# Latent attention swept by halves of 512 queries over two score tiles, instead of quarters of 256 over five

## Chip, core and metric

One NeuronCore of one Trainium2 chip runs the whole kernel as a single program. The metric is device time in microseconds, the median of three runs. The engines are TensorE (PE in the profile, its weight loads PEld), VectorE (DVE), ScalarE (ACT), GpSimd (POOL) and SyncE (SP, which here only issues DMAs).

## What is computed

The kernel is a two-layer encoder on 1024 positions of width 1024, in 32-bit floats. Each layer is a token mixer with four groups of heads, an output projection, and a gated MLP with a short convolution. The change touches group C of the mixer alone, dense latent attention with four heads:

```python
def block(args):
    qn, qr = args
    sc = (jnp.einsum('bqhd,bkhd->bhqk', qn, k_nope) + jnp.einsum('bqhr,bkr->bhqk', qr, k_rope)) * scale
    p = jax.nn.softmax(sc, axis=-1)
    return jnp.einsum('bhqk,bkhd->bqhd', p.astype(v.dtype), v)
...
y = jnp.concatenate([oa, ob, oc, od], axis=-1) @ w_out[l]
```

Every query of a head sees all 1024 keys, with head dimension 96 (64 plain, 32 rotary) and values of 64.

## The kernel before

Activations are kept transposed: channels on the 128 partitions, positions along the free dimension. A matmul that needs full precision is made of three (`mm3`, lines 465 to 470): operands are split into a high part, rounded by ScalarE (line 110), and a low part, the difference, made by GpSimd or VectorE (line 111).

Per layer the mixer runs groups A, D, B and C, then `project_out` multiplies the mixer's 1024 channels, as eight tiles of 128, with the output weights. Group C (`group_c`, 943 to 1003) makes keys for two heads at a time (`keys`) and queries for the next head (`queries`), and sweeps each head in four quarters of 256 queries (`attend_c`, 1005 to 1033). A quarter does this:

- Scores of 8 key tiles x 256 queries, with keys on the partitions, two key tiles to a PSUM bank of 512 columns. ScalarE copies each bank to a score tile `s` in SBUF (line 1021), so `s` is 128 x 2048, 8 KB a partition.
- The maximum over all keys: VectorE folds 2048 columns to 1024, 512 and 256 (1023 to 1025), then `gather` (122 to 134) transposes in 32 x 32 blocks, reduces, and folds the four partition groups with tiny instructions (130 to 133); `replicate` (136 to 138) copies the result back to all groups and `spread` (140 to 144) transposes it into a tile `m` of 256 columns.
- `s - m`: VectorE takes key tiles 0 to 3 and 4 to 6, GpSimd takes key tile 7 (line 1032).
- `weigh` (627 to 639): ScalarE exponentiates 512 columns at a time in place (634); TensorE multiplies with the values, into `o` in PSUM (637). Each weighing matmul is recorded as two. A column block of ones among the values gives the denominators, which `denominators` and `normalise` (641 to 660) use once per head: head h - 1 is finished behind the third quarter of head h, and the last head behind its own end, straight into channel tile 5.

There are five score tiles, used in turn: `self.sc[(4 * h + quarter - 11) % 5]`. They share their SBUF space with the mixer's channel tiles, as `open_shared` (241 to 259) lays out: the pair of high and low part of channel tile k takes 8 KB, and the score tiles lie over the pairs of tiles 1, 3, 7, 4 and 5, in the order in which the last quarters leave them. Tiles 6, 2 and 0 lie over the queries' and keys' low parts and a scratch tile. `mixed()` declares the channel tiles there; a channel tile can be loaded from HBM (line 1087, SyncE's queue) when the score tile under it is no longer read.

`project_out` (1076 to 1116) loads and splits the channel tiles in `ORDER_MIX = (0, 1, 6, 2, 3, 7, 4, 5)`, and first accumulates output tiles 0 to 3 of the first 512 positions over them in that order (`products`, tile `pw`): 8 x 4 x 3 = 96 matmuls, in two `pj` and two `psc` banks. Output tiles 4 to 7 and the second half of the positions follow.

The order on each engine is not written by hand. A planner orders the instructions by their place in the program and by when it expects their inputs; each engine then runs its own list in order and waits on semaphores. Two places bind it: score matmuls are kept in program order (`behind`), and temporaries (`ta` for the maxima, `tb` for the transpose, `tc` for `m`, `tn` for the denominators) exist once each. Score banks are `psc`, two of them; the last head uses the two `pj` banks as well.

Of the kernel before, what the change touches and what calls it, by code (L numbers as in the profile page):

```python
# [9 lines left out]
F32 = mybir.dt.float32  # L10
F32R = mybir.dt.float32r
I32 = mybir.dt.int32
AF = mybir.ActivationFunctionType
ALU = mybir.AluOpType
# [6 lines left out]
S = 1024  # L21
# [42 lines left out]
HALVES = (slice(0, 512), slice(512, 1024))  # L64


ORDER_MIX = (0, 1, 6, 2, 3, 7, 4, 5)
# [25 lines left out]
class Trunk:  # L93
# [147 lines left out]
    def open_shared(self, name):  # L241

        self.hctx = ExitStack()
        p = self.hctx.enter_context(self.tc.tile_pool(name=name, bufs=1, reuse_waits="tile", side="right"))
        half = lambda k, i, dt=F32R: p.tile([128, S], dt, name="hx", tag=f"h{'hl'[i]}{k}")
        pair = lambda k, dt=F32R: p.tile([128, 2 * S], dt, name="hp", tag=f"hp{k}")
        first = (6, 2, 0)
        qlc = [half(6, i) for i in range(2)]
        kls = [half(2, 0), half(2, 1), half(0, 0)]
        rt = half(0, 1, F32)  # L250
        sc = [pair(k, F32) for k in (1, 3, 7, 4, 5)]

        def mixed():
            t = {k: [half(k, i) for i in range(2)] if k in first else
                 (lambda q: [q[:, i * S:i * S + S] for i in range(2)])(pair(k)) for k in ORDER_MIX}
            self.hh, self.hl = ([t[k][i] for k in range(KT)] for i in range(2))

        self.mixed = mixed
        return qlc, kls, rt, sc
# [683 lines left out]
    def group_c(self, l, lat, kr, v, wuk, wuq):  # L943
        nc = self.nc
        (qnh, qnl), ((kvh,), (kvl,)) = lat["cq"], lat["ckv"]
        (ukh, ukl), (uqh, uql), (krh, krl) = wuk, wuq, kr

        def keys(i):
            kh = [(self.lp if i and j else self.kp).tile([128, S], F32R, name="kh", tag="ks") for j in range(2)]
            kl = [next(self.kls) for _ in range(2)]  # L950
            for half in range(2):
                hs = HALVES[half]
                pool, tag = (self.pj, "pj") if i else (self.psc, "psc")
                ps = pool.tile([128, 512], F32, name="pk", tag=tag)
                cs = slice(128 * i, 128 * i + 128)
                self.mm3(ps, ukh[:, cs], ukl[:, cs], kvh[:, hs], kvl[:, hs], True, True)
                for j in range(2):
                    src = ps[64 * j:64 * j + 64]
                    nc.scalar.activation(kh[j][0:64, hs], src, AF.Copy)
                    nc.vector.tensor_sub(kl[j][0:64, hs], src, kh[j][0:64, hs].bitcast(F32))  # L960
            for j in range(2):
                nc.scalar.activation(kh[j][64:128, :], krh[64:128, :].bitcast(F32), AF.Copy)
                nc.vector.tensor_copy(kl[j][64:128, :], krl[64:128, :].bitcast(F32))
            return list(zip(kh, kl))

        def queries(h):
            qh = self.qp.tile([128, S], F32R, name="qh", tag="qh")
            ql = self.qlc[h % 2]
            for half in range(2):
                hs = HALVES[half]  # L970
                ps = self.pj.tile([128, 512], F32, name="pj", tag="pj")
                for k in range(2):
                    cs = slice(512 * k + 128 * h, 512 * k + 128 * h + 128)
                    self.mm3(ps, uqh[:, cs], uql[:, cs], qnh[k][:, hs], qnl[k][:, hs], k == 0, k == 1)

                t = self.rt[half]
                nc.vector.tensor_mul(t, ps, self.cs[:, hs])
                self.split(qh[:, hs], ql[:, hs], t, nc.vector if h == 0 else nc.gpsimd)
            return qh, ql

        ks, qs = keys(0), queries(0)
        end = lambda o, dst=None: self.normalise(dst, o[0:64], 1024, 64 if dst is not None else 0,
                                                 self.denominators(o, 1024))
        last = None
        for h in range(4):
            (kh, kl), (qh, ql) = ks[h % 2], qs
            if h == 1:
                ks = keys(1)
            if h < 3:
                qs = queries(h + 1)  # L990
            o = self.po.tile([128, 1024], F32, name="po", tag="po")
            for quarter in range(4):
                self.attend_c(l, h, quarter, kh, kl, qh, ql, v, o)
                if last and quarter == 2:
                    self.store_mix(448 + 64 * h, end(last))
            last = o

        self.mixed()
        t = self.tmp("b")[64:128]
        end(last, t)  # L1000
        for half in range(2):
            hs = HALVES[half]
            self.split(self.hh[5][64:128, hs], self.hl[5][64:128, hs], t[:, hs], nc.vector)

    def attend_c(self, l, h, quarter, kh, kl, qh, ql, v, o):
        nc = self.nc
        q0 = 256 * quarter
        qs = slice(q0, q0 + 256)
        s = self.sc[(4 * h + quarter - 11) % 5]
        pieces = []  # L1010
        for i in range(4):
            pool, tag = (self.pj, "pj") if i > 1 and h == 3 else (self.psc, "psc")
            ps = pool.tile([128, 512], F32, name="psc", tag=tag)
            for u in range(2):
                kt = 2 * i + u
                ts = slice(128 * kt, 128 * kt + 128)
                with self.behind():
                    self.last = self.mm3(ps[:, 256 * u:256 * u + 256], kh[:, ts], kl[:, ts], qh[:, qs],
                                         ql[:, qs], u == 0, True)
                pieces.append((kt, 256 * kt, slice(256 * kt, 256 * kt + 256), qs))  # L1020
            nc.scalar.activation(s[:, 512 * i:512 * i + 512], ps, AF.Copy)
        mx = self.tmp("a")
        nc.vector.tensor_max(mx, s[:, 0:1024], s[:, 1024:2048])
        nc.vector.tensor_max(mx[:, :512], mx[:, 0:512], mx[:, 512:1024])
        nc.vector.tensor_max(mx[:, :256], mx[:, 0:256], mx[:, 256:512])
        r = self.gather(mx[:, :256], 256, ALU.max)
        self.replicate(r, 8)
        m = self.tmp("c")[:, :256]
        self.spread(m, r[:, :8], 8)
        for eng, c0, c1 in ((nc.vector, 0, 4), (nc.gpsimd, 7, 8), (nc.vector, 4, 7)):  # L1030
            s3 = s[:, 256 * c0:256 * c1].rearrange("p (s q) -> p s q", q=256)
            eng.tensor_sub(s3, s3, m.unsqueeze(1).broadcast_to([128, c1 - c0, 256]))  # L1032
        self.weigh(o, v, h, pieces, s, 2048, 96.0 ** -0.5)


    def mixer(self, l):
# [362 lines left out]
```

## Time and profile before

| | us |
|---|---|
| median of three runs | 3239.51 (3237.86 to 3241.6) |
| the profiled execution | 3236.76 |
| its span, first to last instruction | 3234.9 |
| busy in the span: PE | 2985.9 (92%) |
| DVE | 2029.7 (63%) |
| ACT | 1063.9 (33%) |
| POOL | 956.7 (30%) |
| mean granted TensorE clock, share of full speed | 0.974 |

Busy shares are means over stages with different limits, so the stage of the change has to be cut out by its time. In a list by line, "busy, mean ns" is followed by the idle time ahead of the group and what ended it. In a timeline, an idle time in brackets names the engine and line that ended the wait. A line can be that of a helper: line 126 is the transpose of every `gather`, whoever calls it, so groups are told apart by tile and shape.

### The profile page before, as it was taken

What the parts mean: (1) busy time and instruction counts of PE and PEld (TensorE: products, weight loads), DVE (VectorE), ACT (ScalarE), POOL (GpSimd) and SP (SyncE); (2) the same over time, 40 slices, a digit from 0 to 9 for tenths busy, and PEclk for the clock granted to TensorE, in tenths of its full rate; (3) what the DMA queues carried; (4) which work ended last, traced back from release to release, by engine and by line L of the source; (5) the groups of instructions that cost most, each with busy time, mean ns of one, the idle gap of its engine ahead of it and who ended that gap; (6) DMA issues with size and microseconds to landing.
All of it is one profiled execution on the core that took longest, in us unless ns stands there. A gap on an engine that the chain in (4) does not pass through costs nothing. (4 is left out here: it accounts for less than half of the span.)

```text
span 3234.9 us, 35358 instructions
## 1 busy us (share of the span) xinstructions
PE 2985.9 (92%) x13706; PEld 2365.9 (73%) x13706; DVE 2029.7 (63%) x2849; ACT 1063.9 (33%) x1554; POOL 956.7 (30%) x712
## 2 busy tenths in 40 slices
PE   7888988988999999999988998898899999999997
PEld 3677767776677777788856886777676888888886
DVE  6687567698656666653587727568956434434347
ACT  4232443554332222212243324336534222222222
POOL 1221133324342322223232213142334422233222
PEclk9998999999999999999999998999999999999998
DMA  5235111103312433211131121110132111111113
GB/s 202 78 101 177 54 37 34 56 20 108 128 58 93 134 113 114 95 40 52 46 124 58 55 82 42 38 52 19 37 109 91 65 39 40 43 62 52 40 40 104
DMA packets 103091, 237.15 MB, mean 73 GB/s; under 512 B 11227, under 2 KB 29915, under 8 KB 102924
## 3 DMA queue, kind: packets, MB, share of 16 engines
q1 hardware_dynamic: 102924, 234.90, 22.4%
q8 instruction: 107, 1.75, 0.2%
q14 instruction: 60, 0.49, 0.1%
HBM read 205.59 MB, written 32.67 MB: 74 GB/s over the span
## 5 line engine op out<-in xcount | busy, mean ns | idle before, releaser
L111 POOL TENSOR_TENSOR wl<-raw,wh 128x1024 fp32r<-128x1024 f32 (+2 forms) x96 | 234.5, 2451 | 663.7 <-ACT wh L110 472.4
L477 PE MATMUL pj<-hp,uh 128*128 128x512 f32 x880 | 352.6, 401 | 1.6 <-ACT hp L442 1.6
L478 PE MATMUL pj<-hp,uh 128*128 128x512 f32 x880 | 347.1, 394 | 2.9 <-POOL hp L445 2.8
L477 PE MATMUL pj<-hh,wh 128*128 128x512 f32 x800 | 327.9, 410 | 14.2 <-DVE ql L526 8.5
L478 PE MATMUL pj<-hl,wh 128*128 128x512 f32 x800 | 323.2, 404 | 3.7 <-POOL hl L445 3.2
L481 PE MATMUL pj<-hp,ul 128*128 128x512 f32 x880 | 290.2, 394 | 0.0
L111 POOL TENSOR_TENSOR ul<-raw,uh 128x1024 fp32r<-128x1024 f32 x96 | 238.5, 2486 | 162.5 <-PE pj L481 84.7
L875 DVE TENSOR_SCALAR ta<-u,par 128x1024 f32<-128x1024 f32 (+1 forms) x46 | 55.9, 1216 | 356.1 <-ACT u L1128 324.0
L477 PE MATMUL pj<-hx,uh 128*128 128x512 f32 x528 | 212.5, 403 | 12.6 <-ACT u L1128 10.0
L110 ACT ACTIVATE wh<-raw 128x1024 fp32r<-128x1024 f32 (+2 forms) x104 | 107.2, 1047 | 345.1 <-PE po L469 242.8
L481 PE MATMUL pj<-hx,ul 128*128 128x512 f32 x528 | 209.8, 397 | 0.0
L478 PE MATMUL pj<-hx,uh 128*128 128x512 f32 x528 | 207.7, 393 | 0.0
L481 PE MATMUL pj<-hh,wl 128*128 128x512 f32 x800 | 206.5, 398 | 0.0
L477 PEld LDWEIGHTS pj<-hp,uh 128*128 128x128 f32 x880 | 165.6, 188 | 45.6 <-ACT hp L442 2.2
L478 PEld LDWEIGHTS pj<-hp,uh 128*128 128x128 f32 x880 | 165.5, 188 | 44.9 <-POOL hp L445 5.5
L481 PEld LDWEIGHTS pj<-hp,ul 128*128 128x128 f32 x880 | 165.2, 188 | 39.3 <-issue 1.0
L477 PEld LDWEIGHTS pj<-hh,wh 128*128 128x128 f32 x800 | 154.4, 193 | 54.0 <-issue 17.0
L110 ACT ACTIVATE uh<-raw 128x1024 fp32r<-128x1024 f32 x100 | 105.5, 1059 | 262.9 <-DMA raw<-in_w_up_dram 141.2
L1190 DVE TENSOR_TENSOR y<-y,po 128x1024 f32<-128x1024 f32 x96 | 117.0, 1219 | 110.6 <-PE po L470 110.6
L478 PEld LDWEIGHTS pj<-hl,wh 128*128 128x128 f32 x800 | 154.1, 193 | 41.8 <-POOL hl L445 5.4
L481 PEld LDWEIGHTS pj<-hh,wl 128*128 128x128 f32 x800 | 151.6, 190 | 34.6 <-issue 0.2
L1128 ACT ACTIVATE u<-pj 128x512 f32<-128x512 f32 x176 | 103.7, 593 | 209.1 <-PE pj L481 209.1
(375 smaller groups left out, 7120.2 us busy)
## 6 DMA issues: line engine op xcount, KB each, us to landing
raw<-in_w_up_dram SPq DMA_DIRECT2D x88, 512.0 KB, 3.5
mr<-in_w_mod_dram SPq DMA_DIRECT2D x144, 256.0 KB, 3.4
raw<-in_w_in_dram SPq DMA_DIRECT2D x52, 512.0 KB, 3.5
raw<-in_w_down_dram SPq DMA_DIRECT2D x44, 512.0 KB, 3.5
room<-in_w_mod_dram SPq DMA_DIRECT2D x48, 256.0 KB, 3.6
xd<-y SPq DMA_DIRECT2D x48, 256.0 KB, 2.4
raw<-in_w_out_dram SPq DMA_DIRECT2D x16, 512.0 KB, 3.9
x<-xd SPq DMA_DIRECT2D x14, 512.0 KB, 4.4
```

What stands on the lines that cost most here:

```text
L110: self.nc.scalar.activation(hi, src, AF.Copy)
L111: (eng or self.nc.gpsimd).tensor_sub(lo, src, hi.bitcast(F32))
L477: nc.tensor.matmul(ps, wh[:, ks], self.hh[k][:, hs], start=k == 0, stop=False, skip_group_check=True)
L478: nc.tensor.matmul(ps, wh[:, ks], self.hl[k][:, hs], start=False, stop=False, skip_group_check=True)
L481: nc.tensor.matmul(ps, wl[:, ks], self.hh[k][:, hs], start=False, stop=k == KT - 1, skip_group_check=True)
L875: nc.vector.tensor_scalar(o, t[:, 0:n], cw(0), None, op0=ALU.mult)
L1128: nc.scalar.activation(u[:, 1 + 512 * half:513 + 512 * half], ps, AF.Copy)
L1190: self.mark = nc.vector.tensor_add(d, d, p)
```

## The change

Group C sweeps each head in two halves of 512 queries. A score tile becomes 128 x 4096 (16 KB a partition), and there are two, one for each half of a head. One key tile's scores fill a bank. The maxima are folded as the scores come: after key tile 3 (two blocks of 1024 columns), after 5 and after 7 (one more each), then 1024 to 512. `gather`, `replicate` and `spread` run on 512 queries. VectorE subtracts key tiles 0 to 1, 2 to 3 and 4 to 6, GpSimd key tile 7, now 512 columns. The finished head h - 1 is normalised behind the first half of head h. In the last head only key tiles 5 and 7 use the `pj` banks. The score tiles lie over channel tiles (1, 3) and (7, 4); tile 5 has space of its own.

```diff
-        pair = lambda k, dt=F32R: p.tile([128, 2 * S], dt, name="hp", tag=f"hp{k}")
-        first = (6, 2, 0)
+        quads = ((1, 3), (7, 4))
+        quad = lambda i, dt=F32R: p.tile([128, 4 * S], dt, name="hq", tag=f"hq{i}")
...
-        sc = [pair(k, F32) for k in (1, 3, 7, 4, 5)]
+        sc = [quad(i, F32) for i in range(2)]
...
         def mixed():
-            t = {k: [half(k, i) for i in range(2)] if k in first else
-                 (lambda q: [q[:, i * S:i * S + S] for i in range(2)])(pair(k)) for k in ORDER_MIX}
+            t = {k: [half(k, i) for i in range(2)] for k in (0, 6, 2, 5)}
+            for i, ks in enumerate(quads):
+                q = quad(i)
+                for j, k in enumerate(ks):
+                    t[k] = [q[:, at * S:at * S + S] for at in (2 * j, 2 * j + 1)]
...
-            for quarter in range(4):
-                self.attend_c(l, h, quarter, kh, kl, qh, ql, v, o)
-                if last and quarter == 2:
+            for half in range(2):
+                self.attend_c(l, h, half, kh, kl, qh, ql, v, o)
+                if last and half == 0:
...
+        hs = HALVES[half]
+        s = self.sc[half]
+        pieces, mx = [], self.tmp("a")
+        for kt in range(8):
+            pool, tag = (self.pj, "pj") if kt > 3 and kt % 2 and h == 3 else (self.psc, "psc")
             ps = pool.tile([128, 512], F32, name="psc", tag=tag)
+            ts, cs = slice(128 * kt, 128 * kt + 128), slice(512 * kt, 512 * kt + 512)
+            with self.behind():
+                self.last = self.mm3(ps, kh[:, ts], kl[:, ts], qh[:, hs], ql[:, hs], True, True)
+            nc.scalar.activation(s[:, cs], ps, AF.Copy)
+            pieces.append((kt, 512 * kt, cs, hs))
+            if kt == 3:
+                nc.vector.tensor_max(mx, s[:, 0:1024], s[:, 1024:2048])
+            elif kt in (5, 7):
+                nc.vector.tensor_max(mx, mx, s[:, 512 * kt - 512:512 * kt + 512])
         nc.vector.tensor_max(mx[:, :512], mx[:, 0:512], mx[:, 512:1024])
...
+        r = self.gather(mx[:, :512], 512, ALU.max)
+        self.replicate(r, 16)
+        m = self.tmp("c")[:, :512]
+        self.spread(m, r[:, :16], 16)
+        for eng, c0, c1 in ((nc.vector, 0, 2), (nc.gpsimd, 7, 8), (nc.vector, 2, 4), (nc.vector, 4, 7)):
+            s3 = s[:, 512 * c0:512 * c1].rearrange("p (s q) -> p s q", q=512)
+            eng.tensor_sub(s3, s3, m.unsqueeze(1).broadcast_to([128, c1 - c0, 512]))
+        self.weigh(o, v, h, pieces, s, 4096, 96.0 ** -0.5)
```

## Rows read from the trace of the kernel before

**Rows 1.** Two stretches, busy us (count): PE, PEld, DVE, ACT, POOL; clock; DMA
```profile
630.00:770.00 140.00, 118.70 (x653) 95.22 (x653) 133.54 (x241) 78.74 (x141) 37.70 (x30) 0.96 0.10 29
2210.00:2350.00 140.00, 118.78 (x653) 95.08 (x652) 133.45 (x241) 78.62 (x141) 37.51 (x30) 0.96 0.10 29
```

**Rows 2.** Timeline, PE: start us, us, line, op, tiles [idle before <-releaser]
```profile
777.26 3.69 PE L637 MATMUL po<-hp,v 128*96 128x256 f32 x16 [1.66 <-ACT hp L634]
...
792.88 0.50 PE L469 MATMUL pw<-hp,wh 128*128 128x512 f32 x1 [2.03 <-POOL hp L111]
```

**Rows 3.** Stretches, instructions on pw alone: PE, PEld, ACT busy us (count)
```profile
626.00:780.60 154.60, 11.50 (x43) 7.91 (x44) 0.00 (x0) 0.97 0.12 37
780.60:796.00 15.40, 13.37 (x55) 10.43 (x56) 1.79 (x4) 1.00 0.59 187
```

**Rows 4.** DVE by line and shape, 626 to 772 us: busy us, mean ns
```profile
L1032 DVE TENSOR_TENSOR hp<-hp,tc 128x1024 f32<-128x1024 f32 x15 | 23.0, 1534 | 0.1
L1023 DVE TENSOR_TENSOR ta<-hp 128x1024 f32<-128x1024 f32 x16 | 20.5, 1280 | 0.4 <-ACT hp L1021 0.2
L1032 DVE TENSOR_TENSOR hp<-hp,tc 128x768 f32<-128x768 f32 x15 | 16.9, 1125 | 0.0
L1024 DVE TENSOR_TENSOR ta<-ta 128x512 f32<-128x512 f32 x16 | 12.6, 789 | 0.5
L126 DVE STREAM_TRANSPOSE tb<-ta 128x256 f32<-128x256 f32 x16 | 7.0, 437 | 0.4
L128 DVE TENSOR_REDUCE sm<-tb 128x8 f32<-128x256 f32 x16 | 6.6, 414 | 0.2
L1025 DVE TENSOR_TENSOR ta<-ta 128x256 f32<-128x256 f32 x16 | 6.6, 414 | 0.2
L143 DVE STREAM_TRANSPOSE tc<-sm 128x256 f32<-128x256 f32 x15 | 6.5, 436 | 0.2
L132 DVE COPY sm<-sm 32x8 f32<-32x8 f32 x16 | 5.5, 345 | 0.5
L131 DVE TENSOR_TENSOR sm<-sm 64x8 f32<-64x8 f32 x16 | 4.4, 276 | 0.1
...
L130 DVE COPY sm<-sm 64x8 f32<-64x8 f32 x16 | 2.7, 168 | 0.5
```

**Rows 5.** The same view, 1750 to 2050 us, where halves of 512 run
```profile
L143 DVE STREAM_TRANSPOSE tc<-sm 128x512 f32<-128x512 f32 x6 | 4.1, 691 | 0.2
...
L128 DVE TENSOR_REDUCE sm<-tb 128x16 f32<-128x512 f32 x6 | 4.0, 660 | 0.1
...
L126 DVE STREAM_TRANSPOSE tb<-ta 128x512 f32<-128x512 f32 x5 | 3.5, 703 | 0.1
```

**Rows 6.** Timeline, DVE, first subtraction of a quarter
```profile
642.18 1.77 DVE L1032 TENSOR_TENSOR hp<-hp,tc 128x1024 f32<-128x1024 f32 x1
```

**Rows 7.** Timeline, POOL, the same moment
```profile
642.02 0.85 POOL L1032 TENSOR_TENSOR hp<-hp,tc 128x256 f32<-128x256 f32 x1 [11.12 <-DVE sm L131]
```

**Rows 8.** Timeline, ACT, exponentials of one quarter
```profile
768.43 2.19 ACT L634 ACTIVATE hp<-hp 128x512 f32<-128x512 f32 x4 [7.00 <-DVE hp L1032]
```

**Rows 9.** Timeline, ACT, score copies at the start, [idle before <-releaser]
```profile
636.25 1.30 ACT L1021 ACTIVATE hp<-psc 128x512 f32<-128x512 f32 x2 [0.36 <-PE psc L470]
```

**Rows 10.** Line 1023: duration ns min/median/max, first and last start us
```profile
L1023 DVE TENSOR_TENSOR ta<-hp x32: 1184/1216/2275, 631.7 to 2332.8; 128x1024 f32<-128x1024 f32 x32
```

**Rows 11.** Timeline, DVE, last subtractions, last head's denominators
```profile
775.32 2.62 DVE L1032 TENSOR_TENSOR hp<-hp,tc 128x1024 f32<-128x1024 f32 x2
780.99 1.24 DVE L644 STREAM_TRANSPOSE tn<-po 32x1024 f32<-32x1024 f32 x1 [3.05 <-PE po L637]
```

**Rows 12.** DMA issues by line: KB each, us to landing
```profile
hp<-mixd SPq DMA_DIRECT2D x8, 512.0 KB, 3.6
```

**Rows 13.** Timeline, POOL, low parts after the last weighing
```profile
782.50 2.54 POOL L111 TENSOR_TENSOR hp<-hp 128x512 fp32r<-128x512 f32 x2
785.00 2.40 POOL L111 TENSOR_TENSOR ol<-raw,oh 128x1024 fp32r<-128x1024 f32 x1
```

More of the change, by code (lines that the diff above doesn't have):

```diff
@@ L1003, in group_c, with attend_c @@
             self.split(self.hh[5][64:128, hs], self.hl[5][64:128, hs], t[:, hs], nc.vector)
-    def attend_c(self, l, h, quarter, kh, kl, qh, ql, v, o):
+    def attend_c(self, l, h, half, kh, kl, qh, ql, v, o):
         nc = self.nc
[L1007 to L1012, printed above, removed]
-            ps = pool.tile([128, 512], F32, name="psc", tag=tag)
[L1014 to L1023, printed above, removed]
-        nc.vector.tensor_max(mx[:, :512], mx[:, 0:512], mx[:, 512:1024])
[L1025 to L1033, printed above, removed]
```

## The prediction

> **What bounds the kernel now.** I read first where the changed code runs. Its lines fall in two stretches, one in each layer, about 626 to 781 us and 2206 to 2361 us. The busy time of the engines there [rows 1] says who is late: over 140 us VectorE is busy 133.5, TensorE 118.7, ScalarE 78.7, GpSimd 37.7, and the second layer repeats this within 0.2 us. VectorE has no room; TensorE has some. Right after the stage, in the output projection, TensorE is the full one: 55 matmuls recorded in 15.4 us, one behind the other but for one wait of 2.03 us [rows 2, 3]. So the stage of the change is bound by VectorE, and what follows starts when its last half is weighed and then runs at TensorE's pace. A us that VectorE gives back here moves all that follows forward by a us, if no new wait appears.
>
> Second I read VectorE's list in this stretch, shapes apart [rows 4]: what a quarter costs. Third, the same helpers at 512 queries, which the windowed attention already runs [rows 5]. Then the two ends of the stage, where overlap fails.
>
> **What the change removes on VectorE.** A quarter now costs: maxima 1.280 + 0.789 + 0.414 = 2.483; transpose and reduce 0.437 + 0.414 = 0.851; six tiny copies and maxima of at least 0.168 each, 1.008; the spread 0.436; the two subtractions 1.534 + 1.125 = 2.659 [rows 4]. Sum 7.437, two quarters 14.87 us.
> A half will cost: three maxima of 1024 columns and one of 512, 3 x 1.280 + 0.789 = 4.629; transpose and reduce at 512, 0.703 + 0.660 = 1.363 [rows 5]; again six tiny ones, 1.008; the spread 0.691 [rows 5]; and the subtractions. Those have the same columns as two quarters (3584), in three instructions instead of four. A fixed part per instruction can be read from the transposes: 0.437 at 256 and 0.703 at 512 leave 0.17 at zero. So 2 x 2.659 - 0.17 = 5.148. Sum 12.84.
> The gain is 2.03 us a half, 8 halves a layer: **16.3 us a layer**. Bounds: the tiny instructions are slower than 0.168 on the average (0.276 for the maximum on line 131, 0.345 for the copy on 132 [rows 4]); if the removed ones had cost that, 18.6. If some of the time overlaps in VectorE's pipe, as neighbours that don't depend on each other do, I allow 2 us less, an estimate: 14. I take 16.3, because I read the surplus of the tiny ones as waiting for GpSimd, whose other instructions stay.
>
> That waiting needs its own look, since GpSimd's share grows from 256 to 512 columns an instruction. The first subtraction of a quarter took 1.77 us [rows 6] against 1.28 for the maximum of the same shape, while GpSimd's subtraction ran 0.85 us beside it [rows 7]. I count the hold as growing with GpSimd's instruction, so half as many holds of twice the length: no change. Were the hold a fixed 0.5 us, 8 of 16 would go, 4 us a layer more.
> The Trainium skill (SBUF — State Buffer, "SBUF: two separate sides") says that the port pair that VectorE and GpSimd share is locked for a whole instruction and the loser blocks fully; by that rule the hold grows with the length, and the sum stays. The 0.5 us of hold within a GpSimd instruction of 0.85 agrees.
>
> **TensorE and ScalarE** do the same columns: scores in 512-column matmuls instead of 256, the same count of score copies and exponentials of 512 columns. I cost these at nothing; they hide behind VectorE, with TensorE at 85% of the stretch [rows 1]. If that cover goes, see the rivals.
>
> **Two tiles instead of five.** A tile is free for the next head only when its values are weighed. Start the clock when a half's subtractions start. The first chunk ends at latest at 1.28 plus a hold of 1.0, one exponential takes 0.55 (four take 2.19 [rows 8]), so weighing starts at 2.9; 16 matmuls of a quarter took 3.69 [rows 2], a half 7.4: end at 10.3. The next scores into this tile: two banks per 1.30 + 0.36 us [rows 9], 8 banks 6.6: 16.9, the last copy 17.5. Last maxima 2.1, gather and spread 3.1: the next subtractions of this tile can start at 22.7. VectorE wants them after two halves, 2 x (147 - 16.3) / 8 = 32.7 (147 us, rounded up, from its first maximum at 631.7 [rows 10] to its last subtraction's end at 777.94 [rows 11]). So 10 us of slack: two tiles suffice, as long as TensorE takes the scores of a tile when it is free.
>
> **The ends of the stage.** Fill: the first maximum needs four banks, as now; then two banks come per 1.66 us [rows 9] and a maximum takes 1.28, so VectorE waits twice 0.4: 0.8 (bounds 0 and 2.3, if line 960's work doesn't fill and the last copies come late). Drain: now the last subtractions run 775.32 to 777.94 and the last values are weighed at 780.99 [rows 11], 3.05 later. A half: subtractions 5.15 long, end of weighing at 10.3: 5.15 later. The drain costs **2.1**.
>
> **The handover to the projection.** The score tiles lie where the mixer's channel tiles 1, 3, 7, 4 go. Now tiles 1, 3, 7, 4, 5 come free one after the other, quarter by quarter; then 1 and 3 come free with the last head's first half, 7 and 4 only with the last weighing, 5 at once. By that moment 43 of the 96 first projection matmuls are recorded, 55 after it in 15.4 us with the wait of 2.03 inside [rows 2, 3], 0.24 us each. In the new order channel tile 0 is there early, 1 some 16.3 - 4 - 0.6 - 1.3 = 10 us before the last weighing (load 3.6 to landing [rows 12], high part 0.6, low part on GpSimd 1.27 [rows 13]); in these 10 us TensorE also weighs for 7.4. I take 28 of 96 done: 14 more remain, 3.4 us, less 1.0 for the wait of 2.03, which was for tile 5 and half of which should go: **2.4** (bounds 0 and 5.4). After the last weighing tile 7 comes at 0.3 + 3.6 + 0.6 + 1.3 = 5.8 us, when TensorE has 32 matmuls, 7.8 us, still to do: no new wait. Loads queued behind these two on SP are those of the later output weights, wanted 15 us after.
>
> **Sum.** A layer: 16.3 - 0.8 - 2.1 - 2.4 = 11.0 us; two layers 22.0. The profiled execution took 3236.8 us (span 3234.9), which gives 3214.8; it lies 2.7 below the median of the runs, 3239.5, so the forecast is **3217.5**. Its own range: best 18.6 - 2.1 - 0.8, twice, 31 off: 3208; worst 14 - 2.3 - 2.1 - 5.4, twice, 8 off: 3231.
>
> **Rivals.**
> *Two tiles are too few (slower).* TensorE works in order. If the planner puts the scores of a free tile behind the weighing of the other half, they start at 16.3 + 10.3 = 26.6 instead of 10.3, the tile is ready for subtraction at 39.0 instead of 22.7, and VectorE, which wants it at 32.7, waits 6.3 per pair of halves. Three reuses a layer per tile pair: 19 us, and 11.0 turns to -8: two layers, 3255. It decides from 3.7 us of wait per pair (11.0 / 3). Against: weighing waits for the exponentials now too, 1.66 us for the last one [rows 2], and a planner that sees such a gap has scores ready to fill it, and there are 10 us of slack. For: with five tiles a free one was always there, so the trace of before shows no order for this case.
> The Trainium skill (Perfetto Trace Analysis, "Optimization Strategy") says that the same gap repeating on the engine that should be full can mean too few buffers for the next tile; by it this rival's gap would repeat six times in all. The trace of before shows no such gap on VectorE, but it has five tiles.
> *The gain is lost at the handover (no change).* GpSimd makes the low parts of tiles 7 and 4 and of the output weights, 2.40 each [rows 13]. With four weights queued ahead of tile 7, it comes at 5.8 + 9.6 = 15.4 and TensorE, out of work at 7.8, idles 7.6: 3.4 a layer left, 3233; with the 5.4 of the upper bound above, 3239. This is also where the change could fail to do what it says: VectorE is faster but the stage's successor doesn't start sooner. For: after the last weighing GpSimd now runs such things back to back for 4.9 us [rows 13]. Against: the planner may take them in either order.
> *More than forecast.* The holds shrink too, 4 us a layer more, 15.0 twice: 3209.5; with the upper bound of the tiny ones, 2.3 more twice: 3205.
>
> **Chances.** Forecast 0.55, more than that 0.13, handover 0.17, too few tiles 0.15. 0.2% is 6.5 us, about what a measurement of this kernel can tell from no change. Faster by over that: 0.68; within: 0.17; slower: 0.15. Range for 8 in 10: the forecast, the better case and the handover case, 3204 to 3241.
>
> **What would show it.** Right: VectorE still over 90% busy in a stretch that is 11 to 15 us shorter; maxima of 512-query halves at the prices above; the last weighing about 5 us after the last subtraction; TensorE continuous from there but for small waits. Wrong: gaps on VectorE ahead of a maximum, ended by score copies; ScalarE's score copies waiting for TensorE's weighing; a wait of TensorE for GpSimd's low parts of tiles 7 or 4 of more than 3 us; weighing matmuls that are dearer per column at 512 than at 256.

## The result, and the profile after

The changed kernel takes 3293.55 us (median of four, 3289.16 to 3298.36) against 3239.78 us for the kernel before beside it: a ratio of 1.0169, 95% interval 1.0155 to 1.0183. It is 54 us slower, where 22 us faster was forecast. The profiled execution has a span of 3287.4 us, 52.5 more than the 3234.9 before, and a mean granted clock of 0.964 against 0.974.

The first view is the busy time in stretches of layer 0 and layer 1, columns as in [rows 1], with two short stretches in which TensorE waits for much of the time. The window in layer 1 begins before its stage, since all is later by then:

```profile
630.00:770.00 140.00, 105.51 (x320) 55.10 (x318) 103.10 (x133) 71.57 (x127) 32.13 (x17) 0.89 0.06 18
2210.00:2350.00 140.00, 105.69 (x348) 59.61 (x347) 109.38 (x146) 74.56 (x132) 38.17 (x17) 0.88 0.06 19
...
690.00:710.00 20.00, 13.24 (x26) 5.01 (x27) 12.52 (x16) 9.50 (x18) 7.81 (x2) 0.72 0.06 14
...
770.00:790.00 20.00, 7.69 (x13) 2.83 (x14) 19.56 (x21) 6.37 (x11) 15.11 (x7) 0.66 0.26 85
```

VectorE, busy 133.5 of 140 us in [rows 1], is busy 103.1 here, and TensorE fell with it. Nothing is full any more: the engines wait for each other. VectorE's list by line and shape, 626 to 800 us, says what its work costs and where it waits (busy us, mean ns | idle before, releaser):

```profile
L1032 DVE TENSOR_TENSOR hq<-hq,tc 128x1024 f32<-128x1024 f32 x16 | 27.0, 1724 | 0.1
L1024 DVE TENSOR_TENSOR ta<-ta,hq 128x1024 f32<-128x1024 f32 x16 | 20.5, 1284 | 3.7 <-ACT hq L1019 3.4
L1032 DVE TENSOR_TENSOR hq<-hq,tc 128x1536 f32<-128x1536 f32 x8 | 14.0, 1745 | 0.0
L1022 DVE TENSOR_TENSOR ta<-hq 128x1024 f32<-128x1024 f32 x8 | 9.8, 1222 | 1.9 <-ACT hq L1019 1.7
...
L126 DVE STREAM_TRANSPOSE tb<-ta 128x512 f32<-128x512 f32 x8 | 5.6, 694 | 0.1
L128 DVE TENSOR_REDUCE sm<-tb 128x16 f32<-128x512 f32 x8 | 5.4, 681 | 0.2
L1025 DVE TENSOR_TENSOR ta<-ta 128x512 f32<-128x512 f32 x8 | 5.4, 677 | 0.2
L647 DVE STREAM_TRANSPOSE tn<-po 32x1024 f32<-32x1024 f32 x4 | 5.0, 1244 | 34.0 <-PE po L640 34.0
```

The maxima and subtractions cost what was predicted. The four `denominators` (line 647) are preceded by 34.0 us of idle time, all of it for TensorE's weighing. The timelines show the cycle that makes these waits: VectorE, then TensorE, then ScalarE (start us, us, instruction, [idle before <-releaser]).

```profile
671.86 1.24 DVE L647 STREAM_TRANSPOSE tn<-po 32x1024 f32<-32x1024 f32 x1 [7.33 <-PE po L640]
...
690.38 4.01 DVE L1032 TENSOR_TENSOR hq<-hq,tc 128x1024 f32<-128x1024 f32 x3
...
697.79 5.11 DVE L1032 TENSOR_TENSOR hq<-hq,tc 128x1024 f32<-128x1024 f32 x3
712.97 1.25 DVE L647 STREAM_TRANSPOSE tn<-po 32x1024 f32<-32x1024 f32 x1 [10.08 <-PE po L640]
715.06 1.23 DVE L1022 TENSOR_TENSOR ta<-hq 128x1024 f32<-128x1024 f32 x1 [0.84 <-ACT hq L1019]
...
732.37 3.98 DVE L1032 TENSOR_TENSOR hq<-hq,tc 128x1024 f32<-128x1024 f32 x3
...
754.44 1.24 DVE L647 STREAM_TRANSPOSE tn<-po 32x1024 f32<-32x1024 f32 x1 [9.97 <-PE po L640]
...
799.98 1.24 DVE L647 STREAM_TRANSPOSE tn<-po 32x1024 f32<-32x1024 f32 x1 [6.57 <-PE po L640]
```

```profile
696.75 16.18 PE L640 MATMUL po<-hq,v 128*96 128x512 f32 x32 [12.38 <-ACT hq L637]
712.37 0.79 PE L471 MATMUL psc<-qh,kh 128*128 128x512 f32 x1
...
738.71 15.69 PE L640 MATMUL po<-hq,v 128*96 128x512 f32 x32 [12.40 <-ACT hq L637]
...
782.31 9.21 PE L640 MATMUL po<-hq,v 128*96 128x512 f32 x16 [13.05 <-ACT hq L637]
792.84 7.11 PE L640 MATMUL po<-hq,v 128*96 128x512 f32 x16 [1.32 <-ACT hq L637]
...
803.89 0.79 PE L472 MATMUL pw<-hq,wh 128*128 128x512 f32 x1 [2.21 <-POOL hq L111]
```

```profile
695.55 4.27 ACT L637 ACTIVATE hq<-hq 128x512 f32<-128x512 f32 x8 [10.79 <-POOL hq L1032]
...
822.82 0.60 ACT L1104 ACTIVATE y<-pw 128x512 f32<-128x512 f32 x1 [11.84 <-PE pw L473]
```

In the two middle heads TensorE weighs both halves in one run of 32 matmuls. Then, from 712.37 on, it takes 48 score matmuls: those of the next head, whose first two key tiles already stood in the two banks, and the first two key tiles of the head after. While it weighs there are no further scores, and VectorE runs out of work: it waits 10.1 us, until 712.97. While VectorE makes the maxima and subtracts, TensorE waits: 12.4 us. The engines take turns (the texts written before the runs call this lockstep). One turn, from a half's subtraction to that of the same tile in the next head, lasts 732.37 - 690.38 = 42.0 us: 6.4 until weighing starts, 16.2 of weighing, 19.4 from the denominators to the subtraction.

The end of the stage is late by more. The last denominators are at 799.98 instead of 780.99 [rows 11], 19.0 us later. The first copy of an output tile out of `pw` is at 822.82; ScalarE's timeline of the kernel before has it here:

```profile
793.64 0.60 ACT L1104 ACTIVATE y<-pw 128x512 f32<-128x512 f32 x1 [2.82 <-PE pw L470]
```

That is 29.2 us later, so the handover costs 10.2 more (22.84 against 12.65). By the same copy in layer 1 (2427.05 against 2373.37) both layers together lose 53.7 us: the whole difference lies in these two stages.

### The profile page after: what moved, and what is told of

Its sections match the earlier page's. It is cut to its first block, busy times and chain, and to the rows that moved or that the text cites. A ratio compares the mean times of both kernels' runs of the same rounds, so it can differ in the third digit from the quotient of the medians.

```text
span 3287.4 us, 33858 instructions
## 1 busy us (share of the span) xinstructions
PE 2987.8 (91%) x13066; PEld 2293.5 (70%) x13066; DVE 2001.6 (61%) x2657; ACT 1064.9 (32%) x1554; POOL 971.8 (30%) x696
## 5 line engine op out<-in xcount | busy, mean ns | idle before, releaser
L480 PE MATMUL pj<-hx,uh 128*128 128x512 f32 x704 | 282.0, 401 | 9.2 <-ACT u L1128 6.6
L480 PE MATMUL pj<-hq,uh 128*128 128x512 f32 x704 | 282.4, 401 | 1.6 <-ACT hq L445 1.6
L481 PE MATMUL pj<-hq,uh 128*128 128x512 f32 x704 | 277.6, 394 | 1.0 <-POOL hq L448 1.0
L481 PE MATMUL pj<-hx,uh 128*128 128x512 f32 x704 | 276.4, 393 | 1.8 <-POOL hx L448 1.8
L484 PE MATMUL pj<-hx,ul 128*128 128x512 f32 x704 | 250.2, 396 | 0.0
L484 PE MATMUL pj<-hq,ul 128*128 128x512 f32 x704 | 249.3, 395 | 0.0
L640 PE MATMUL po<-hq,v 128*96 128x512 f32 x256 | 130.2, 669 | 86.7 <-ACT hq L637 86.7
L471 PE MATMUL po<-ah,wh 128*128 128x512 f32 x432 | 171.3, 397 | 0.0
L472 PE MATMUL po<-al,wh 128*128 128x512 f32 x432 | 170.7, 395 | 0.0
```

The lines of the kernel that those rows point to most:

```text
L471: nc.tensor.matmul(ps, wh, xh, start=first, stop=False, skip_group_check=True)
L472: nc.tensor.matmul(ps, wh, xl, start=False, stop=False, skip_group_check=True)
L480: nc.tensor.matmul(ps, wh[:, ks], self.hh[k][:, hs], start=k == 0, stop=False, skip_group_check=True)
L481: nc.tensor.matmul(ps, wh[:, ks], self.hl[k][:, hs], start=False, stop=False, skip_group_check=True)
L484: nc.tensor.matmul(ps, wl[:, ks], self.hh[k][:, hs], start=False, stop=k == KT - 1, skip_group_check=True)
L640: nc.tensor.matmul(o[0:96, co], v(tt, h), s[:, cs], start=co.start // 512 not in seen, stop=False, skip_group_check=True)
```

## The experiments

| kernel | ratio to the kernel before | 95% interval |
|---|---|---|
| changed kernel | 1.0169 | 1.0155 to 1.0183 |
| scores ahead of weighing | 0.9986 | 0.9976 to 0.9995 |
| nothing subtracted on GpSimd | 1.0079 | 1.0061 to 1.0096 |
| GpSimd's exponential last | 1.0084 | 1.0067 to 1.0101 |
| other mixing order | 1.0117 | 1.0101 to 1.0132 |
| before, two of its five tiles | 1.0242 | 1.0223 to 1.0261 |
| before, four of its five tiles | 1.0005 | 0.9995 to 1.0014 |
| before, two tiles, scores ahead | 1.0082 | 1.0059 to 1.0105 |
| before, nothing subtracted on GpSimd | 0.9996 | 0.9986 to 1.0005 |
| scores ahead, nothing on GpSimd | 0.9947 | 0.9932 to 0.9962 |
| the same, other mixing order | 0.9941 | 0.9919 to 0.9962 |
| scores ahead, GpSimd's exponential last | 0.9933 | 0.9918 to 0.9948 |

**1. Is it the order on TensorE?** The same two tiles, but the next half's scores are put into TensorE's list ahead of this half's weighing: `attend_c` is cut into scores, softmax and weighing, and the weighing is tied behind the last score matmul.

```diff
-                self.attend_c(l, h, half, kh, kl, qh, ql, v, o)
+                unit = self.scores_c(l, h, half, kh, kl, qh, ql)
+                if todo:
+                    todo()
...
+                todo = self.soften_c(h, half, unit, v, o)
...
+        def weigh():
+            with self.behind():
+                self.weigh(o, v, h, pieces, s, 4096, 96.0 ** -0.5)
+        return weigh
```

> The changed kernel, with the score matmuls of the next half put ahead of the weighing of the present half on TensorE (order weigh n-1, scores n+1, weigh n), nothing else. Lockstep theory (with two tiles the planner puts both weighings of a head ahead of the next head's scores, VectorE runs dry for 7 to 10 us a head): the waits of VectorE for TensorE ahead of the denominators fall under 3 us, three heads a layer, so 30 to 60 us come back: 3235 to 3262. GpSimd theory (the loss is the first exponential of a half, which waits for GpSimd's slowed subtraction): less than 10 us come back, 3283 to 3293. Handover theory (the loss is at the projection): nothing comes back in the stage, 3290.

Measured 3239.01 us, ratio 0.9986: all of the loss is gone with the tiles, the widths and the prices unchanged. TensorE's waits for exponentials ahead of group C's weighing fall from 86.7 us in the whole kernel to 4.2. So the order was the main cause. But it only comes level with the kernel before; the gain on VectorE is still missing. VectorE's last subtraction ended at 771.65, 6.3 us before that of [rows 11], and yet its denominators are hardly earlier. In TensorE's list projection matmuls of channel tile 1 stand ahead of the last weighing. One of them waits 4.28 us for GpSimd's low part, so the weighing starts only at 771.96:

```profile
780.36 1.24 DVE L647 STREAM_TRANSPOSE tn<-po 32x1024 f32<-32x1024 f32 x1 [8.71 <-PE po L640]
```
```profile
770.08 0.80 PE L472 MATMUL pw<-hq,wh 128*128 128x512 f32 x1 [4.28 <-POOL hq L111]
771.96 8.37 PE L640 MATMUL po<-hq,v 128*96 128x512 f32 x16
```

In the halves before, ScalarE holds things up: an exponential that stands first waits for GpSimd, and score copies stand behind it. TensorE now waits 24.3 us in the whole kernel for such copies to empty its score banks; with GpSimd's exponential last (experiment 5) it is 8.1.

```profile
698.65 0.63 ACT L637 ACTIVATE hq<-hq 128x512 f32<-128x512 f32 x1 [2.33 <-POOL hq L1042]
...
713.19 1.15 ACT L637 ACTIVATE hq<-hq 128x512 f32<-128x512 f32 x2 [5.82 <-POOL hq L1042]
```

**2. Is it the number of tiles or their size?** In the kernel before, quarters of 256, two of the five tiles in use; and four, the same space as the change has.

```diff
-        s = self.sc[(4 * h + quarter - 11) % 5]
+        s = self.sc[3 + quarter % 2]
```
```diff
-        s = self.sc[(4 * h + quarter - 11) % 5]
+        s = self.sc[1 + quarter]
```

> The kernel before, quarters of 256, with two of its five 8 KB score tiles in use. Lockstep theory (the number of tiles, not the width of a sweep, makes the order): the planner pairs two weighings and then two quarters of scores; a pair then takes 7.4 of weighing + 6.6 of scores + some 9 from the last score to the first exponential = 23 us against 18.3 now, 7 pairs a layer: about 3290 to 3315. Width theory (halves of 512 are the cause): as before, 3235 to 3245.

> The kernel before with four of its five 8 KB score tiles in use: the same score space as the changed kernel's, in four pieces. Lockstep theory: a free tile is nearly always there, order stays mixed, within 10 us of the kernel before: 3232 to 3250. If the space counts and not the number of pieces: as slow as the changed kernel, 3280 to 3300.

Two tiles: 3320.80 us, ratio 1.0242, a little over the 3290 to 3315 of the lockstep theory. Four: 3244.36, ratio 1.0005, as it had it. The same space cut in four costs nothing that can be measured; two tiles make the turns, without the wider sweep. TensorE's timeline with two small tiles has the same pattern, two quarters weighed in one run after a wait:

```profile
675.73 8.83 PE L637 MATMUL po<-hp,v 128*96 128x256 f32 x32 [4.76 <-ACT hp L634]
697.77 9.98 PE L637 MATMUL po<-hp,v 128*96 128x256 f32 x32 [6.59 <-ACT hp L634]
724.27 8.69 PE L637 MATMUL po<-hp,v 128*96 128x256 f32 x32 [9.95 <-ACT hp L634]
```

**3. Does the cure help there too?** The edit of the first experiment, made to the kernel before with two of its tiles.

```diff
-        s = self.sc[(4 * h + quarter - 11) % 5]
+        s = self.sc[3 + quarter % 2]
...
+                unit = self.scores_c(l, h, quarter, kh, kl, qh, ql)
+                if todo:
+                    todo()
```

> The kernel before (quarters of 256 queries) with two of its five 8 KB tiles in use, as in the run of two small tiles (3320.8), and the cure of the scores ahead: each quarter's scores stand ahead of the quarter before's weighing on TensorE. If two tiles cost time only through the order that they lead to, it comes back to 3238 to 3255, level with five tiles. If two tiles are too few by themselves (a tile's next scores still wait for its weighing), half or more of the 80 us stays: 3280 to 3320. Against the halves with the scores ahead and the exponential last (3223.0) it also says what the width gives between kernels with two tiles and the same order: the forecast's 11 us a layer would make it 3245.

Measured 3267.30 us, ratio 1.0082: two thirds of the loss come back (1.0242 to 1.0082), and neither theory had this right. TensorE's waits for exponentials go from 105.4 us to 57.8, where the kernel before has 41.7. Two small tiles stay too few in this order too, while two tiles twice as long suffice to come level. That a quarter gives TensorE only half the time to fill the other tile would explain it; that is argued, not shown.

**4. What does GpSimd's share cost?** Key tile 7 is subtracted by VectorE too, first in the changed kernel, then in the kernel before.

```diff
-        for eng, c0, c1 in ((nc.vector, 0, 2), (nc.gpsimd, 7, 8), (nc.vector, 2, 4), (nc.vector, 4, 7)):
+        for eng, c0, c1 in ((nc.vector, 0, 2), (nc.vector, 2, 4), (nc.vector, 4, 8)):
```
```diff
-        for eng, c0, c1 in ((nc.vector, 0, 4), (nc.gpsimd, 7, 8), (nc.vector, 4, 7)):
+        for eng, c0, c1 in ((nc.vector, 0, 4), (nc.vector, 4, 8)):
```

> The changed kernel, with GpSimd's subtraction (key tile 7) given to VectorE, so that no exponential waits for GpSimd. GpSimd theory: the exponentials of a head's first half start 1.5 us after the subtractions instead of 5; some 4 us a head, 8 heads, less 0.5 us of VectorE a half: 3265 to 3275, and if it were the whole loss 3240. Lockstep theory: the order of TensorE stays two weighings, then two halves of scores, so VectorE still waits over 6 us a head; only the chain's piece in front of the weighing shrinks: not under 3262.

> The kernel before with the GpSimd share of the subtraction given to VectorE (two subtractions of four key tiles a quarter). If the 25 us that this edit gave back in the changed kernel come from its exponentials standing in an order in which the first of a half waits for GpSimd, it gives nothing here, where key tiles 6 and 7 share one exponential that comes last: 3238 to 3256 (VectorE has more to do). If GpSimd's share costs by itself, through the held port, it gives back up to 20 us here too: 3220 to 3235.

Measured 3267.98 us, ratio 1.0079, and 3240.90 us, ratio 0.9996. Half of the loss comes back in the changed kernel, nothing in the kernel before. So it isn't GpSimd's subtraction as such. The first time lies in the range of the GpSimd theory, and the bound of the lockstep theory, not under 3262, holds too: what the exponentials wait for and the turns both have a part in the loss. What differs is the order of the exponentials: before, key tiles 6 and 7 share one, the last of four. After, key tile 7 has one of its own, and the planner puts it first, so the other seven stand behind it. GpSimd's timeline of the changed kernel shows how late that can be (a long and a short case):

```profile
690.03 5.49 POOL L1032 TENSOR_TENSOR hq<-hq,tc 128x512 f32<-128x512 f32 x1 [3.50 <-DVE tc L143]
697.83 2.31 POOL L1032 TENSOR_TENSOR hq<-hq,tc 128x512 f32<-128x512 f32 x1 [2.31 <-DVE tc L143]
```

The first ends at 695.52, VectorE's three at 694.39, and all eight exponentials start at 695.55.

**5. The order, or the two engines holding each other up?** GpSimd keeps its share, and only its exponential is moved from first to last; in the changed kernel, and with the scores ahead.

```diff
-            nc.scalar.activation(s[:, at:at + w], s[:, at:at + w], AF.Exp, scale=scale)
+            late = at == 3584 and n == 4096
+            with self.tc.issue_after(ex.ins) if late else ExitStack():
+                ex = nc.scalar.activation(s[:, at:at + w], s[:, at:at + w], AF.Exp, scale=scale)
```

> The changed kernel with its key tile 7, which GpSimd subtracts, kept on GpSimd, but with that key tile's exponential put last of the eight in ScalarE's order instead of first. Theory that the 25 us that came back when GpSimd's share went to VectorE are owed to the order (seven exponentials stand behind one that waits for GpSimd): 20 to 28 us less than the changed kernel, 3266 to 3274. Rival that they are owed to the two engines holding each other up while both subtract: within 5 us of 3293.6, since the last exponential then waits as long as the first did.

> The kernel with the scores ahead, and the exponential of GpSimd's key tile put last. If the order is the cause, this comes out with the run in which VectorE subtracts everything, 3220 to 3229, with GpSimd still at work; if the holding is, it stays with the scores ahead alone, 3235 to 3243.

Measured 3271.83 us, ratio 1.0084, and 3222.95 us, ratio 0.9933. The order is the cause: the intervals overlap with those of the runs without GpSimd's share (1.0079 and 0.9947). GpSimd's subtraction is as long as ever, but ScalarE starts 3.9 us earlier:

```profile
690.08 5.51 POOL L1034 TENSOR_TENSOR hq<-hq,tc 128x512 f32<-128x512 f32 x1 [3.49 <-DVE tc L143]
```
```profile
691.68 2.29 ACT L639 ACTIVATE hq<-hq 128x512 f32<-128x512 f32 x4 [6.88 <-DVE hq L1034]
694.54 2.19 ACT L639 ACTIVATE hq<-hq 128x512 f32<-128x512 f32 x4 [0.58 <-DVE hq L1034]
```

With both orders mended (below: the mended kernel) it beats either order mended alone, and the kernel before. In VectorE's timeline of that run the waits for weighing are gone but for the last, and TensorE's weighing comes in pieces of one half, never waiting more than 2.2 us for exponentials:

```profile
691.67 5.11 DVE L1044 TENSOR_TENSOR hq<-hq,tc 128x1024 f32<-128x1024 f32 x3
...
704.82 5.10 DVE L1044 TENSOR_TENSOR hq<-hq,tc 128x1024 f32<-128x1024 f32 x3
709.95 1.25 DVE L649 STREAM_TRANSPOSE tn<-po 32x1024 f32<-32x1024 f32 x1
...
721.47 5.12 DVE L1044 TENSOR_TENSOR hq<-hq,tc 128x1024 f32<-128x1024 f32 x3
...
755.97 6.18 DVE L1044 TENSOR_TENSOR hq<-hq,tc 128x1024 f32<-128x1024 f32 x3
770.09 1.24 DVE L649 STREAM_TRANSPOSE tn<-po 32x1024 f32<-32x1024 f32 x1 [7.94 <-PE po L642]
```
```profile
682.00 7.03 PE L642 MATMUL po<-hq,v 128*96 128x512 f32 x16
696.62 7.03 PE L642 MATMUL po<-hq,v 128*96 128x512 f32 x16
```

**6. The handover.** The changed kernel with its mixing blocks in another order, which puts tiles 6 and 2, which don't lie under the score tiles, ahead of tile 1; and the scores ahead with VectorE subtracting everything, in the old and in this order.

```diff
-ORDER_MIX = (0, 1, 6, 2, 3, 7, 4, 5)
+ORDER_MIX = (0, 6, 2, 1, 3, 7, 4, 5)
```

> The changed kernel with one thing altered: the order of the mixing blocks, so that output channel tile 0's second block comes second and the rest keep to the two inputs already loaded (0, 6, 2, 1, 3, 7, 4, 5). Handover theory (the stretch from the last denominators to the first output copy, 22.8 us against 12.65, is owed to the order in which TensorE's idle time at the end of the last half can be filled): 8 to 12 us less than the changed kernel's 3293.6, so 3281 to 3286. Lockstep theory alone (the handover only hands on what the last half is late by): within 3 us of 3293.6.

> As the run with the scores ahead and the subtraction all on VectorE, with the mixing order of the changed kernel: against the run with the scores ahead alone (3239.0) it says what the GpSimd share costs when there is no lockstep. The theory that the late exponentials hold up the last half's weighing: 3220 to 3235. The theory that VectorE's busy time sets the stage: 3240 to 3255.

> The changed kernel with three edits: the next half's scores stand ahead of this half's weighing on TensorE, VectorE does the subtraction of key tile 7 too (none on GpSimd), and the mixing order of the run before. If the three causes are separate and each costs what it cost alone (54 us lockstep; some of the 25 us that the GpSimd share cost, here the 3 to 6 us a half by which exponentials wait for it; 8 to 12 us handover), it runs at 3205 to 3230, faster than both kernels. If VectorE bounds the stage once the scores are ahead, the added subtraction (0.8 to 1 us a half by the rows, 16 us in all) eats what the earlier exponentials give: 3235 to 3250.

Measured 3279.69 us, ratio 1.0117: 14 us back by the times and some 17 by the ratios, as the handover theory had it and more than its 8 to 12. The first output copy now comes 15.5 us after the last denominators at 798.31, not 22.8:

```profile
813.77 0.60 ACT L1104 ACTIVATE y<-pw 128x512 f32<-128x512 f32 x1 [4.45 <-PE pw L473]
```

In the changed kernel TensorE has all but one matmul of tile 0 behind it at 769 and stands until the weighing at 782: tiles 6 and 2 come after tile 1 in its list, and tile 1 isn't there. In the other order it runs 15 matmuls of the next two blocks in that gap. With the scores ahead the order is worth nothing that can be told: 3224.76 (0.9947) and 3222.55 us (0.9941), with intervals that overlap. The second lies in the range that was given for three separate causes, but this one adds nothing there, so they aren't separate. So the longer handover was mostly a debt of the turns: TensorE's free time lay where only tile 0 was there. SyncE's queue in the changed kernel shows the loads of the score-tile channels at 796, behind three loads of weights, and at 803, behind two of the input:

```profile
784.40 11.59 SPq L116 DMA_DIRECT2D raw<-in_w_out_dram  x3
796.09 0.86 SPq L1087 DMA_DIRECT2D hq<-mixd  x2
799.30 3.72 SPq L460 DMA_DIRECT2D raw<-in_x_dram  x2
803.12 0.88 SPq L1087 DMA_DIRECT2D hq<-mixd  x2
```

A version with three tiles of 16 KB wasn't tried: it would take 48 KB a partition, where the five tiles of before take 40 and the two take 32.

## Why the prediction was wrong, by its own steps

**What bounds the kernel: right for before, and it stopped being so.** VectorE bounds the stage while the other engines have scores and weighed values ready. After the change none is full.

**VectorE's prices: right.** Subtractions 41.0 us for eight halves, 5.12 each, against 5.148 worked out; maxima 4.46 against 4.63; transpose and reduce 1.37 against 1.36. Only the six tiny ones were too cheap, 1.85 a half against 1.01; those of two quarters were too, 2.96 against 2.02, so that the difference is right by luck. Over the whole kernel VectorE is busy 28.1 us less (2029.7 to 2001.6), 14.0 a layer, and 32.9 less (1996.8), 16.4 a layer, in the kernel with both orders mended: the term was 16.3 with bounds 14 and 18.6. The gain was there, but in the changed kernel it became idle time.

**GpSimd's hold: right for VectorE, blind for GpSimd.** The hold on VectorE grew with the length: VectorE's three subtractions took 5.11 us where it was held and 4.01 where it wasn't, 1.1 a half, against 0.5 a quarter in [rows 6]. The Trainium skill (SBUF — State Buffer, "SBUF: two separate sides") has it so, too. Neither the rows nor the step asked how long GpSimd is held and who waits for it. With the exponential of its key tile standing first, that costs 27 us in the changed kernel (1.0169 to 1.0084) and 17 us with the scores ahead (0.9986 to 0.9933).

**TensorE and ScalarE at nothing: wrong once the cover went.** The columns are the same, but a weighing that follows a long wait runs slower: 9.21 us for 16 matmuls after 13.05 us of wait, in a stretch with a granted clock of 0.66, and 16.18 for 32 in one of 0.72, against 7.03 for 16 in the mended kernel, where the engine is kept busy. Four runs (8.80, 16.18, 15.69, 9.21 against 7.03 or 14.06) make 7.7 us a layer of the turns' length. These clocks are means of 20 us, so a part of each stretch was at the lower level, 1.2 GHz, and in [rows 1] the mean is 0.96.

**Two tiles instead of five: the step that failed.** It worked out 10 us of slack "as long as TensorE takes the scores of a tile when it is free". It didn't: the planner put the scores of both tiles, but for two banks of them, behind the weighing of both. VectorE stood idle for 34.0 us of layer 0 ahead of the denominators. The rival named this mechanism and got its turn nearly right (39.0 us for a tile from subtraction to subtraction, 42.0 measured), but two things were wrong with it. Its price took VectorE's own pace as 32.7 us for two halves; with the orders mended it is 29.8 (721.47 - 691.67) at this place, so the turn of 42.0 loses 12, not 6.3. And its chance of 0.15 rested on "a planner that sees such a gap has scores ready to fill it", for which no row stood. That the trace of before couldn't show the order with two tiles was said; it spoke for two cases nearly as likely as each other. The rule cited there (the Trainium skill, Perfetto Trace Analysis, "Optimization Strategy") agrees: the gap repeats three times a layer, 7.3, 10.1 and 10.0 us. But more buffers were not the only remedy: with the same two, the order closed it. Of the signs of being wrong that were named, the gap on VectorE came, but ahead of the denominators and ended by weighing, more than ahead of a maximum (34.0 us against 5.6).

**Fill: right.** 0.65 and 0.42 us of wait at the first maxima in the mended kernel, 1.1 in all, where 0.8 was forecast.

**Drain: too small.** Last subtraction to last weighing is 3.05 before [rows 11], 6.6 after and 7.9 in the mended kernel; 5.15 was forecast. In the mended kernel, as with the scores ahead alone (experiment 1), TensorE waits 4.2 us for a low part of GpSimd ahead of the last weighing. The drain step had no projection matmuls in front of it.

**Handover: right size in the mended kernel, wrong in the changed one.** 2.4 was forecast, with 28 of the 96 first projection matmuls done by the last weighing; 11 were in the changed kernel and 20 in the mended one, by those recorded. The cost is 10.2 with the turns, 2.8 with the other mixing order (15.5 against 12.65), and 3.1 in the mended kernel (15.8). The rival's cause, GpSimd's low parts, isn't what made it long in the changed kernel: TensorE's longest wait for one there is 2.21 us.

**The sum.** In the changed kernel, layer 0, the stretch from the first maximum to the end of the last subtraction is 161.3 us, against 146.2 before: 15.1 longer, where 15.5 shorter was forecast. With 3.5 more of drain and 10.2 of handover that is 28.8 of the 29.2 us lost there. In the mended kernel the stretch is 128.9, 17.3 shorter; 4.9 of drain and 3.1 of handover leave 9.3, where 11.0 was forecast, and layer 1 gives 7.9 in the same way. By the ratio, 0.9933, the mended kernel is 22 us faster, which is the forecast's number; the terms of the traces make 17, so the agreement is in part luck. The forecast priced the change with an order on TensorE and ScalarE that the change, as it is made, doesn't have. That the 22 are all owed to the halves isn't shown: the mended kernel also has other orders than the kernel before, and no run gives these to the kernel before with its five tiles.

## What to carry to other kernels

When buffers become fewer, write out each engine's list for one turn in the order in which it may really run, and price both orders: with two buffers, one engine that finishes both before it refills either makes the engines take turns. Try the order before more space: here it gave all of the loss back, and with two small tiles two thirds. When a piece of shared work goes to a slower or held engine, look at what stands behind the instruction that waits for it, in that one's engine's list; put that instruction last. Matmuls behind a long wait were dearer here, up to 9.21 us for 7.03, so a wait on TensorE should be priced with the slower rows of the trace.

## What the runs showed of the hardware

Who holds whom, when GpSimd and VectorE subtract at the same time, isn't fixed. In the changed kernel GpSimd's 128 x 512 lasted 1.29, about 2.3 or 5.49 us. In the first half of a layer and in a later one it started 0.38 and 0.35 us ahead of VectorE's three; in the first it lasted 1.29 and VectorE's three 5.87, in the later one 5.49 and 4.01. The 5.87 can't all be put down to that subtraction: from 649.72 on GpSimd made a low part for the queries, and with nothing subtracted on GpSimd (scores ahead) VectorE's three still took 5.59 at this place:

```profile
648.47 1.29 POOL L1032 TENSOR_TENSOR hq<-hq,tc 128x512 f32<-128x512 f32 x1 [17.12 <-DVE tc L143]
```
```profile
648.85 5.87 DVE L1032 TENSOR_TENSOR hq<-hq,tc 128x1024 f32<-128x1024 f32 x3
```

The later one ended 1.13 us after the last of VectorE's three (695.52 against 694.39), about as long as the shortest takes, so it seems to have waited for all three. The Trainium skill (SBUF — State Buffer, "SBUF: two separate sides") gives the pair of ports to whichever starts first, for that instruction. The first case agrees; in the later one, and in two more like it in that layer, the engine that began first by the trace lost, and over three instructions. Spans on GpSimd are rough, and what decides it stays open.

VectorE alone with all eight key tiles (scores ahead, nothing on GpSimd) took this in the middle heads:

```profile
673.86 4.56 DVE L1042 TENSOR_TENSOR hq<-hq,tc 128x1024 f32<-128x1024 f32 x3
```

It is 4.56 us for eight key tiles, between the 4.01 and 5.11 for seven beside GpSimd in the changed kernel, and less than the 5.10 to 5.12 for seven in the mended one. There the share on GpSimd bought VectorE nothing.
